# Instance normalisation over rows of 4096: an unrolled, tile-scheduled program rewritten as loops of three tiles with hand-placed semaphores

## Chip, cores, metric

One core of a Trainium2 chip. The metric is the time of one execution on the device in microseconds. A run is one execution; a median is over several. Runs of one call share a chip.

## The reference

```python
x: (256, 256, 4096) float32, eps = 1e-5
mean = np.mean(x, axis=2, keepdims=True)
var  = np.var(x, axis=2, keepdims=True)
return (x - mean) / np.sqrt(var + eps)
```

There are 65,536 rows. 1073.74 MB are read and as many written.

## The kernel before

A tile is 512 rows, four per partition, 64 KB in each of 128 partitions (8.39 MB). Three tiles are held at a time. Tile t is loaded, VectorE sums its rows, ScalarE squares the deviations and takes roots, both scale the tile in place, and it is stored. The last tile is cut in two. SyncE issues all transfers on one queue.

```python
K = 4; BUFS = 3
io = ctx.enter_context(tc.tile_pool(name="io", bufs=BUFS))
...
def load(i):
    x_tile = io.tile([P, K, d], fp32)
    keep(nc.sync.dma_start(out=x_tile[:, : spans[i][1], :], in_=rows(x_flat, spans[i])))
...
def mean(r):
    keep(nc.vector.tensor_reduce(out=part[:, r, :], in_=row, axis=AX.X, op=ALU.add))
    ...
# the order of issue
for i in range(BUFS):
    load(i)
for i in range(last + 1):
    compute(i)
    if i == last - 2:
        load(last)
    store(i)
    if 1 <= i < last - 2:
        load(i + 2)
```

The program is written out in full: 128 tiles, 2436 VectorE instructions.

## Time and profile before

| | before |
|---|---|
| median of the first three runs | 5013.53 us (5005.49 to 5014.84) |
| profiled run | 4995.86 us |
| VectorE, ScalarE busy | 68%, 50% |
| moved | 2147.5 MB, mean 430 GB/s |
| instruction fetch (queue 14) | 38 transfers, 0.31 MB |

The **busy share** is the time that transfers took over the time there was. The **rate** counts bytes. This is the line of rates in 40 slices of the page of before:

```profile
GB/s 426 430 433 431 434 434 432 435 435 433 433 436 434 433 434 433 434 432 432 429 428 433 431 429 433 429 430 429 434 425 427 428 429 429 427 428 428 428 433 391
```

### The profile page before, as it was taken

How to read it: one execution, taken by the hardware profiler on the slowest of the kernel's cores; microseconds unless marked ns; L12 is line 12 of the kernel's file. 1: busy time of each engine (PE TensorE's matmuls, PEld its weight loads, DVE VectorE, ACT ScalarE, POOL GpSimd, SP SyncE). 2: the span in 40 equal slices, each digit the busy share in tenths (PEclk: the TensorE clock that was granted, in tenths of full speed). 3: DMA queues.
4: the chain of work that ended last, by engine and by line, in shares of the span. 5: the costliest groups of instructions: out<-in, count | busy, mean ns of one | idle time of the engine just before them, and what ended most of it. 6: DMA issues, size and time to landing. Idle time of an engine off the chain costs nothing.

```text
span 4994.1 us, 4917 instructions
## 1 busy us (share of the span) xinstructions
DVE 3392.6 (68%) x2436; ACT 2501.4 (50%) x1413; POOL 0.2 (0%) x4
## 2 busy tenths in 40 slices
DVE  6666667766776667666667666766666666666666
ACT  4555445554455445554455544555445554455545
POOL 0000000000000000000000000000000000000000
DMA  9999999999999999999999999999999999999999
GB/s 426 430 433 431 434 434 432 435 435 433 433 436 434 433 434 433 434 432 432 429 428 433 431 429 433 429 430 429 434 425 427 428 429 429 427 428 428 428 433 391
DMA packets 37190, 2147.81 MB, mean 430 GB/s; under 512 B 4128, under 2 KB 4128, under 8 KB 4128
## 3 DMA queue, kind: packets, MB, share of 16 engines
q1 hardware_dynamic: 37152, 2147.50, 99.9%
q14 instruction: 38, 0.31, 0.0%
HBM read 1073.74 MB, written 1073.74 MB: 430 GB/s over the span
## 4 chain that ended last, share of the span: by engine, by line
DVE 53%; DMA 23%; another core or an unknown queue 20%; ACT 3%; issue 1%; SPq 0%; ACTq 0%
DVE part L74 37%; DMA x_tile<-in_x_dram 22%; DVE x_tile L95 12%; DVE nsum L75 2%; ACT junk L81 2%; ACT x_tile L103 2%; DVE nmean L76 1%; DMA out_dram<-x_tile 1%; DVE nbias L89 1%; DVE rstd L88 0%; SPq L118 0%; ACTq L159 0%; ACT L87 0%; ACT std L87 0%
## 5 line engine op out<-in xcount | busy, mean ns | idle before, releaser
L74 DVE TENSOR_REDUCE part<-x_tile 128x64 f32<-128x4096 f32 x512 | 2258.8, 4412 | 1520.3 <-DMA x_tile<-in_x_dram 1520.3
L81 ACT ACTIVATE junk<-x_tile,nmean 128x4096 f32<-128x4096 f32 x512 | 1883.0, 3678 | 2445.2 <-DVE nmean L76 2445.2
L95 DVE TENSOR_SCALAR x_tile<-x_tile,rstd,nbias 128x4096 f32<-128x4096 f32 x383 | 912.6, 2411 | 10.4 <-DVE nbias L89 1.1
L103 ACT ACTIVATE x_tile<-x_tile,nbias,rstd 128x4096 f32<-128x4096 f32 x129 | 488.5, 3787 | 0.1
L75 DVE TENSOR_REDUCE nsum<-part 128x1 f32<-128x64 f32 x512 | 112.7, 220 | 17.7
L81 ACT ACTIVATION_READ_ACCUMULATOR junk<-x_tile,nmean 128x1 f32 x512 | 95.5, 187 | 0.0
L76 DVE TENSOR_SCALAR nmean<-nsum 128x1 f32<-128x1 f32 x512 | 78.7, 154 | 17.5
L87 ACT ACTIVATE std<-ss,eps_tile 128x3 f32<-128x3 f32 (+1 forms) x258 | 76.2, 295 | 8.3
L88 DVE RECIPROCAL rstd<-std 128x3 f32<-128x3 f32 (+1 forms) x258 | 41.6, 161 | 8.6 <-ACT std L87 8.6
L89 DVE TENSOR_TENSOR nbias<-nmean,rstd 128x3 f32<-128x3 f32 (+1 forms) x258 | 41.5, 161 | 8.9
L81 ACT ACT_TABLE_LOAD x1 | 1.3, 1283 | 22.7 <-DMA x_tile<-in_x_dram 22.7
L87 ACT ACT_TABLE_LOAD x1 | 1.3, 1283 | 0.0
L49 DVE MEMSET eps_tile<- 128x1 f32 x1 | 0.1, 59 | 0.8 <-PEq L145 0.8
L145 POOL MEMSET const-bfloat16-1.0<- 128x1 bf16 x1 | 0.1, 102 | 0.0
L145 POOL MEMSET const-uint8-127<- 128x1 uint8 x1 | 0.1, 102 | 0.0
L145 POOL MEMSET const-float32-0.0<- 128x1 f32 x1 | 0.1, 99 | 0.2 <-issue 0.2
L145 POOL MEMSET const-float32-1.0<- 128x1 f32 x1 | 0.1, 99 | 0.0
## 6 DMA issues: line engine op xcount, KB each, us to landing
x_tile<-in_x_dram SPq DMA_DIRECT2D x2, 4096.0 KB, 30.7
out_dram<-x_tile SPq DMA_DIRECT2D x2, 4096.0 KB, 18.9
x_tile<-in_x_dram SPq DMA_DIRECT2D x127, 50.4
out_dram<-x_tile SPq DMA_DIRECT2D x127, 31.1
```

Source lines behind the costliest of these rows:

```text
L49: nc.vector.memset(eps_tile, eps)
L74: keep(nc.vector.tensor_reduce(out=part[:, r, :], in_=row, axis=AX.X, op=ALU.add))
L75: keep(nc.vector.tensor_reduce(out=nsum[:, c], in_=part[:, r, :], axis=AX.X, op=ALU.add, negate=True))
L76: keep(nc.vector.tensor_scalar_mul(out=nmean[:, c], in0=nsum[:, c], scalar1=1.0 / d))
L81: nc.scalar.activation(out=junk, in_=x_tile[:, r, :], func=AF.Square, bias=nmean[:, c], scale=1.0, accum_out=ss[:, c])
L87: keep(nc.scalar.activation(out=std[:, c], in_=ss[:, c], func=AF.Sqrt, bias=eps_tile, scale=1.0 / d))
L88: keep(nc.vector.reciprocal(out=rstd[:, c], in_=std[:, c]))
L89: keep(nc.vector.tensor_mul(out=nbias[:, c], in0=nmean[:, c], in1=rstd[:, c]))
L95: nc.vector.tensor_scalar(out=row, in0=row, scalar1=rstd[:, c], scalar2=nbias[:, c], op0=ALU.mult, op1=ALU.add)
L103: keep(nc.scalar.activation(out=row, in_=row, func=AF.Identity, bias=nbias[:, c], scale=rstd[:, c]))
L145: nc = _bacc.Bacc("TRN2", target_bir_lowering=False, num_devices=1)
```

## The change

The intent is a short program: each engine runs a loop over three tiles, waits on semaphores placed by hand, and the waiter resets each one, so that rounds need no barrier. Computation and its order stay. The core of the diff, cut:

```diff
-    io = ctx.enter_context(tc.tile_pool(name="io", bufs=BUFS))
+    X = [pool.tile([P, K, d], fp32, name=f"x{s}") for s in range(BUFS)]
+    loaded = [nc.alloc_semaphore(f"loaded{s}") for s in range(BUFS)]
...
+    def take(engine, sem, count):
+        engine.wait_ge(sem, count)
+        engine.sem_clear(sem)
...
+    def store(s, k, dst):
+        take(S, done[s], k)
+        S.dma_start(out=dst, in_=X[s][:, :k, :]).then_inc(stored[s], 16)
+    def load(s, k, src):
+        take(S, stored[s], 16)
+        S.dma_start(out=X[s][:, :k, :], in_=src).then_inc(loaded[s], 16)
...
-    for i in range(BUFS):
-        load(i)
-    for i in range(last + 1):
-        compute(i)
-        ...
+                load(0, K, x_t[0])
+                load(1, K, x_t[1])
+                with S.Fori(0, rounds * BUFS, BUFS) as i:
+                    for s in range(BUFS):
+                        store(s, K, out_t[bass.ds(i + s, 1)]...)
+                        load((s + 2) % BUFS, K, x_t[bass.ds(i + s + 2, 1)]...)
...
+                with V.Fori(0, rounds) as i:
+                    for s in range(BUFS):
+                        vector_tile(s, K)
...
+                with A.Fori(0, rounds) as i:
+                    for s in range(BUFS):
+                        scalar_tile(s, K)
```

Besides what it intends, the change loads two tiles at the start instead of three, and puts the tiles at byte 16544 of a partition instead of 16512.

More of the change, by code (lines that the diff above doesn't have):

```diff
@@ L18 @@
     nc = tc.nc
-    keep = tc.keep_in_program_order
     fp32 = mybir.dt.float32
@@ L32 @@
     assert n % (P * K) == 0 and d % C == 0
-    spans = [(t * P * K, K) for t in range(n // (P * K) - 1)]
-    spans += [(n - P * K, K // 2), (n - P * K // 2, K // 2)]
-    last = len(spans) - 1
-    def rows(flat, span):
-        r0, k = span
-        return flat[r0 : r0 + P * k, :].rearrange("(p k) d -> p k d", k=k)
-    io = ctx.enter_context(tc.tile_pool(name="io", bufs=BUFS))
-    small = ctx.enter_context(tc.tile_pool(name="small", bufs=4))
-    singles = ctx.enter_context(tc.tile_pool(name="singles", bufs=1))
+    ntiles = n // (P * K)
@@ L46 @@
+    x_t = x_flat.rearrange("(t p k) d -> t p k d", p=P, k=K)
+    out_t = out_flat.rearrange("(t p k) d -> t p k d", p=P, k=K)
+    half = K // 2
+    h0 = n - P * K
+    x_h = x_flat[h0:n, :].rearrange("(h p k) d -> h p k d", p=P, k=half)
+    out_h = out_flat[h0:n, :].rearrange("(h p k) d -> h p k d", p=P, k=half)
+    pool = ctx.enter_context(tc.tile_pool(name="pool", bufs=1))
     psum = ctx.enter_context(tc.tile_pool(name="psum", bufs=1, space=bass.MemoryType.PSUM))
-    eps_tile = singles.tile([P, 1], fp32)
@@ L49 @@
-    nc.vector.memset(eps_tile, eps)
+    eps_tile = pool.tile([P, 1], fp32)
     junk = psum.tile([P, d], fp32)
-    tiles = {}
-    def load(i):
-        x_tile = io.tile([P, K, d], fp32)
-        keep(nc.sync.dma_start(out=x_tile[:, : spans[i][1], :], in_=rows(x_flat, spans[i])))
-        tiles[i] = x_tile
-    def compute(i):
-        x_tile = tiles[i]
-        k = spans[i][1]
-        part = small.tile([P, K, C], fp32)
-        nsum = small.tile([P, K], fp32)
-        nmean = small.tile([P, K], fp32)
-        ss = small.tile([P, K], fp32)
-        std = small.tile([P, K], fp32)
-        rstd = small.tile([P, K], fp32)
-        nbias = small.tile([P, K], fp32)
-        def mean(r):
-            c = slice(r, r + 1)
-            row = x_tile[:, r, :].rearrange("p (c f) -> p c f", c=C)
-            keep(nc.vector.tensor_reduce(out=part[:, r, :], in_=row, axis=AX.X, op=ALU.add))
-            keep(nc.vector.tensor_reduce(out=nsum[:, c], in_=part[:, r, :], axis=AX.X, op=ALU.add, negate=True))
-            keep(nc.vector.tensor_scalar_mul(out=nmean[:, c], in0=nsum[:, c], scalar1=1.0 / d))
-        def square(r):
-            c = slice(r, r + 1)
-            keep(
-                nc.scalar.activation(
-                    out=junk, in_=x_tile[:, r, :], func=AF.Square, bias=nmean[:, c], scale=1.0, accum_out=ss[:, c]
-                )
-            )
-        def scales(c):
-            keep(nc.scalar.activation(out=std[:, c], in_=ss[:, c], func=AF.Sqrt, bias=eps_tile, scale=1.0 / d))
-            keep(nc.vector.reciprocal(out=rstd[:, c], in_=std[:, c]))
-            keep(nc.vector.tensor_mul(out=nbias[:, c], in0=nmean[:, c], in1=rstd[:, c]))
-        def apply_dve(r):
-            c = slice(r, r + 1)
-            row = x_tile[:, r, :]
-            keep(
-                nc.vector.tensor_scalar(
-                    out=row, in0=row, scalar1=rstd[:, c], scalar2=nbias[:, c], op0=ALU.mult, op1=ALU.add
-                )
-            )
-        def apply_act(r):
-            c = slice(r, r + 1)
-            row = x_tile[:, r, :]
-            keep(nc.scalar.activation(out=row, in_=row, func=AF.Identity, bias=nbias[:, c], scale=rstd[:, c]))
-        for r in range(k - 1):
-            mean(r)
-            square(r)
-        mean(k - 1)
-        scales(slice(0, k - 1))
-        square(k - 1)
-        for r in range(k - 2):
-            apply_dve(r)
-        scales(slice(k - 1, k))
-        apply_dve(k - 1)
-        apply_act(k - 2)
@@ L117, in store @@
-    def store(i):
-        keep(nc.sync.dma_start(out=rows(out_flat, spans[i]), in_=tiles.pop(i)[:, : spans[i][1], :]))
-    for i in range(BUFS):
-        load(i)
-    for i in range(last + 1):
-        compute(i)
-        if i == last - 2:
-            load(last)
-        store(i)
-        if 1 <= i < last - 2:
-            load(i + 2)
+    X = [pool.tile([P, K, d], fp32, name=f"x{s}") for s in range(BUFS)]
+    part = [pool.tile([P, K, C], fp32, name=f"part{s}") for s in range(BUFS)]
+    nsum, nmean, ss, std, rstd, nbias = (
+        [pool.tile([P, K], fp32, name=f"{name}{s}") for s in range(BUFS)]
+        for name in ("nsum", "nmean", "ss", "std", "rstd", "nbias")
+    )
@@ new lines @@
+    loaded = [nc.alloc_semaphore(f"loaded{s}") for s in range(BUFS)]
+    stored = [nc.alloc_semaphore(f"stored{s}") for s in range(BUFS)]
+    own_v = nc.alloc_semaphore("own_v")
+    own_a = nc.alloc_semaphore("own_a")
+    means = nc.alloc_semaphore("means")
+    stds = nc.alloc_semaphore("stds")
+    scaled = nc.alloc_semaphore("scaled")
+    done = [nc.alloc_semaphore(f"done{s}") for s in range(BUFS)]
+    ready = nc.alloc_semaphore("ready")
+    def take(engine, sem, count):
+        engine.wait_ge(sem, count)
+        engine.sem_clear(sem)
@@ new lines, with vector_tile, mine @@
+    V, A, S = nc.vector, nc.scalar, nc.sync
+    def vector_tile(s, k):
+        x = X[s]
+        own = 0
+        def mine(instruction):
+            nonlocal own
+            own += 1
+            return instruction.then_inc(own_v, 1)
+        take(V, loaded[s], 16)
+        for r in range(k):
+            c = slice(r, r + 1)
+            row = x[:, r, :].rearrange("p (c f) -> p c f", c=C)
+            mine(V.tensor_reduce(out=part[s][:, r, :], in_=row, axis=AX.X, op=ALU.add))
+            V.wait_ge(own_v, own)
+            mine(V.tensor_reduce(out=nsum[s][:, c], in_=part[s][:, r, :], axis=AX.X, op=ALU.add, negate=True))
+            V.wait_ge(own_v, own)
+            V.tensor_scalar_mul(out=nmean[s][:, c], in0=nsum[s][:, c], scalar1=1.0 / d).then_inc(means, 1)
+        for i, c in enumerate((slice(0, k - 1), slice(k - 1, k))):
+            if i == 0:
+                V.wait_ge(stds, 1)
+            else:
+                take(V, stds, 2)
+            mine(V.reciprocal(out=rstd[s][:, c], in_=std[s][:, c]))
+            V.wait_ge(own_v, own)
+            mine(V.tensor_mul(out=nbias[s][:, c], in0=nmean[s][:, c], in1=rstd[s][:, c]))
+            if i == 0:
+                V.wait_ge(own_v, own)
+                V.sem_inc(scaled, 1)
+            else:
+                take(V, own_v, own)
+            for r in range(0, k - 2) if i == 0 else (k - 1,):
+                c = slice(r, r + 1)
+                V.tensor_scalar(
+                    out=x[:, r, :], in0=x[:, r, :], scalar1=rstd[s][:, c], scalar2=nbias[s][:, c],
+                    op0=ALU.mult, op1=ALU.add,
+                ).then_inc(done[s], 1)
@@ new lines, in scalar_tile @@
+    def scalar_tile(s, k):
+        x = X[s]
+        for r in range(k):
+            c = slice(r, r + 1)
+            if r == k - 1:
+                A.wait_ge(own_a, k - 1)
+                A.activation(
+                    out=std[s][:, : k - 1], in_=ss[s][:, : k - 1], func=AF.Sqrt, bias=eps_tile, scale=1.0 / d
+                ).then_inc(stds, 1)
+                take(A, means, k)
+            else:
+                if r:
+                    A.wait_ge(own_a, r)
+                A.wait_ge(means, r + 1)
+            A.activation(
+                out=junk, in_=x[:, r, :], func=AF.Square, bias=nmean[s][:, c], scale=1.0, accum_out=ss[s][:, c]
+            ).then_inc(own_a, 1)
+        take(A, own_a, k)
+        c = slice(k - 1, k)
+        A.activation(out=std[s][:, c], in_=ss[s][:, c], func=AF.Sqrt, bias=eps_tile, scale=1.0 / d).then_inc(stds, 1)
+        c = slice(k - 2, k - 1)
+        take(A, scaled, 1)
+        A.activation(
+            out=x[:, k - 2, :], in_=x[:, k - 2, :], func=AF.Identity, bias=nbias[s][:, c], scale=rstd[s][:, c]
+        ).then_inc(done[s], 1)
@@ new lines, in store, with _ @@
+    def store(s, k, dst):
[4 more added lines that the diff above has]
+        S.dma_start(out=X[s][:, :k, :], in_=src).then_inc(loaded[s], 16)
+    rounds = (ntiles - 4) // BUFS
+    tail = [(t % BUFS, K, x_t[t], out_t[t]) for t in range(rounds * BUFS, ntiles - 1)]
+    tail += [((ntiles - 1 + h) % BUFS, half, x_h[h], out_h[h]) for h in range(2)]
+    with tc.tile_critical():
+        with nc.Block() as block:
+            @block.sync
+            def _(sync):
+                for s in range(BUFS):
+                    S.sem_inc(stored[s], 16)
+                load(0, K, x_t[0])
+                load(1, K, x_t[1])
+                with S.Fori(0, rounds * BUFS, BUFS) as i:
+                    for s in range(BUFS):
+                        store(s, K, out_t[bass.ds(i + s, 1)].rearrange("o p k d -> p (o k) d"))
+                        load((s + 2) % BUFS, K, x_t[bass.ds(i + s + 2, 1)].rearrange("o p k d -> p (o k) d"))
+                todo = tail[2:]
+                for t, (s, k, _, dst) in enumerate(tail):
+                    if t == len(tail) - 3:
+                        load(*todo.pop(0)[:3])
+                    store(s, k, dst)
+                    if todo:
+                        load(*todo.pop(0)[:3])
+                for s in range(BUFS):
+                    take(S, stored[s], 16)
+            @block.vector
+            def _(vector):
+                V.memset(eps_tile, eps).then_inc(ready, 1)
+                with V.Fori(0, rounds) as i:
+                    for s in range(BUFS):
+                        vector_tile(s, K)
+                for s, k, _, _ in tail:
+                    vector_tile(s, k)
+            @block.scalar
+            def _(scalar):
+                take(A, ready, 1)
+                with A.Fori(0, rounds) as i:
+                    for s in range(BUFS):
+                        scalar_tile(s, K)
+                for s, k, _, _ in tail:
+                    scalar_tile(s, k)
```

## The prediction

> **What bounds the kernel now.** I read the page from the top: busy shares, slices, queues, chain, groups; then the chain in order of time for the middle of the run, the timeline of the SP queue there, and the timeline of the first 120 us.
>
> The head of the page, its slices and its queues:
>
> ```profile
> span 4994.1 us, 4917 instructions
> DVE 3392.6 (68%) x2436; ACT 2501.4 (50%) x1413; POOL 0.2 (0%) x4
> DMA  9999999999999999999999999999999999999999
> DMA packets 37190, 2147.81 MB, mean 430 GB/s; under 512 B 4128, under 2 KB 4128, under 8 KB 4128
> q1 hardware_dynamic: 37152, 2147.50, 99.9%
> q14 instruction: 38, 0.31, 0.0%
> ```
>
> No engine is near full: VectorE stands at 68%, ScalarE at 50%. The row of nines and the 99.9% say that the 16 DMA engines have work throughout; 1073.74 MB in and the same out cannot be made smaller by this change. The kernel is a copy of 2147.5 MB at 430 GB/s with the arithmetic beside it. The chain of waits gives VectorE 53%, but it follows what released what and does not see a FIFO behind a busy wire; the group table shows what VectorE does between tiles:
>
> ```profile
> L74 DVE TENSOR_REDUCE part<-x_tile 128x64 f32<-128x4096 f32 x512 | 2258.8, 4412 | 1520.3 <-DMA x_tile<-in_x_dram 1520.3
> L95 DVE TENSOR_SCALAR x_tile<-x_tile,rstd,nbias 128x4096 f32<-128x4096 f32 x383 | 912.6, 2411 | 10.4 <-DVE nbias L89 1.1
> ```
>
> VectorE waits 1520.3 us for loads, over 126 waits 12.1 us a tile. The timeline in the middle of the run shows where that wait sits:
>
> ```profile
> 2518.42 0.33 SPq L118 DMA_DIRECT2D out_dram<-x_tile  x1
> 2518.80 0.43 SPq L57 DMA_DIRECT2D x_tile<-in_x_dram  x1
> 2530.01 4.42 DVE L74 TENSOR_REDUCE part<-x_tile 128x64 f32<-128x4096 f32 x1 [11.71 <-DMA x_tile<-in_x_dram]
> ...
> 2557.06 0.33 SPq L118 DMA_DIRECT2D out_dram<-x_tile  x1
> 2557.44 0.43 SPq L57 DMA_DIRECT2D x_tile<-in_x_dram  x1
> 2568.96 4.42 DVE L74 TENSOR_REDUCE part<-x_tile 128x64 f32<-128x4096 f32 x1 [12.01 <-DMA x_tile<-in_x_dram]
> ```
>
> One tile takes 38.95 us (2530.01 to 2568.96). A tile is 128 x 16384 x 4 = 8.39 MB each way, which is 19.5 us a transfer and 39.0 us a tile at 430 GB/s: the period is the traffic. From a tile's landing to its store's issue are 27.05 us (2530.01 to 2557.06). When a store is issued, the next load still needs 11.5 to 11.9 us to land. So the queue never runs dry, and **each tile has about 11.5 us of slack**: whatever the change adds between landing and store is hidden up to that.
>
> [...] a load's median time to landing is 50.4 us, which is the remaining 11.5 plus store 19.5 plus itself 19.5. [...] The listing of the built program has loop bodies of 71 instructions on VectorE, 40 on ScalarE and 20 on SyncE[...]. [...]
>
> **The change part by part.**
>
> 1. Unrolled program becomes loops. The instruction queue moved 0.31 MB; at 430 GB/s that is 0.7 us of wire. Removing most of it: -0.7 us. [...]
>
> 2. Semaphores. Per tile VectorE gets three wait-and-clear instructions and one separate increment; ScalarE three wait-and-clears and two split waits; SyncE two wait-and-clears and two fused address calculations. None was in the trace; my estimate is at most 0.2 us each (the shortest recorded operation, the mean's scaling at 154 ns, is the scale). Even were all 13 in series: 2.6 us, inside 11.5: 0. The waits on the engine's own work were there before, in the same places.
>
> 3. Activation tables. The built listing has two table loads inside ScalarE's loop body, before the first square and before the first root, where the unrolled program has two in all. At 1.28 us (the page's row) that is 82 x 1.28 = 105 us more ScalarE busy time, about 2606 us. The first of each round falls while ScalarE waits for VectorE's first mean (it sat idle 17 us there). The second lies between third square and root: it may delay every third tile by up to 1.3 us. With part 2 that is 3.9 us at worst, inside 11.5: 0.
>
> 4. **Start.** This isn't in the words of the change. Before issues three loads at once, then store 0. The changed program issues loads 0 and 1, then waits for tile 0, stores it, and only then issues load 2. The beginning of the trace of before:
>
> ```profile
> 0.73 1.34 SPq L57 DMA_DIRECT2D x_tile<-in_x_dram  x3
> 22.62 4.42 DVE L74 TENSOR_REDUCE part<-x_tile 128x64 f32<-128x4096 f32 x1 [21.77 <-DMA x_tile<-in_x_dram]
> 50.50 27.22 SPq L118 DMA_DIRECT2D out_dram<-x_tile  x2
> ```
>
> Load 0 needs 21.8 us on an empty queue (0.73 to 22.57), 2.3 more than its 19.5 of wire: start-up and completion. Load 1 lands at 22.6 + 19.5 = 42.1. In before load 2 then fills the wire to 61.6, past the store issued at 50.50. In the changed kernel nothing follows load 1; the store on an empty queue lands at 50.5 + 21.8 = 72.3 instead of 42.1 + 19.5 = 61.6. **The wire stands idle for 10.7 us.** From there the order is the same (store 0, load 2, store 1, load 3, ...), the slack of every tile is again 39.0 - 28 = 11, and nothing makes the gap up: the wire is the bound, and time lost on it is lost. +10.7 us. [...]
>
> 5. End. The last loads and stores have constant addresses and the order of before; at 4977.7, when the last store is issued, the wire still had about 5 us of the store ahead to do (the last store landed 15.5 us later for 9.8 us of wire). The extra semaphore work is hidden there. [...]
>
> Sum: -0.7 + 10.7 + 0.8 + 1.2 = +12.0 us. 5013.53 + 12.0 = 5025.5, taken as 5025.
>
> **The rivals.**
> - The compute chain becomes the bound. For: a store's address now comes from registers, waits are separate instructions, tables reload. Against: 11.5 us of slack, against 3.9 at worst. A loss of 2% is 100 us over 128 tiles, 0.8 us a tile beyond the slack, so 12.3 us of additions. Time then: over 5115. Chance 2%.
> - The transfer itself gets slower. The build puts the tiles at byte 16544 of a partition instead of 16512, so at a multiple of 32 rather than of 128, and a register address might give other descriptors. Against: the listing has the same shape, 128 rows of 64 KB, on the same queue[...]. A loss of 2% would show as 421 GB/s in all slices. Time then 5115. Chance 2 to 3%.
> - The start costs nothing, because the missing load is made up later. For: the queue holds 11 us of work in reserve. Against: reserve only prevents idling; it does not move bytes sooner. Time then 5014.
> - Removing the long program helps: [...] a tile lands only with its slowest engine. 0.31 MB on one engine of 27 GB/s would be 11.5 us, which could cancel the start. Against: 99.9% busy on all sixteen shows no engine waiting for a slow one. Time then 5014 as well. These two I give 20% together; they make the low side of the range.
>
> **Range and chances.** The three runs before lie from 5005 to 5015 and the profiled one took 4995.86, so a run moves by some 10 us either way. Centre 5025; low 5008 (rival three or four and a good run), high 5045 (the gap doubled by a slow entry or longer first tile, and a poor run). Two per cent is 100 us either way: faster is all but ruled out[...]; slower needs the first or second rival.
>
> **What would show it.** In the profile of the changed kernel: GB/s near 430 in all slices but the first; the first slice a tenth lower (10.7 of its 125 us); the first store issued at about 51 us and load 2 right behind it rather than at the start; VectorE's first wait for tile 2 long, until about 92 us; later waits for loads 9 to 12 us a tile (a wait near zero would show the compute chain as the bound, and be my error); table loads x82 or slightly more; instruction-queue bytes far below 0.31 MB. The prediction is wrong if the middle period is not 38.9 us, or if the start gap is there while the end does not move.

Three terms lose their lines: the branches (0), entering the block (+0.8) and leaving it (+1.2); the last two were the author's estimates, not worked out from a trace. The sum came to -0.7 + 10.7 + 0.8 + 1.2 = +12.0 us, so 5025; without the two it would be +10.0, so 5023.5. The 27 GB/s of one engine in the last rival is the page's 430 over 16 engines. Of the 2.3 us that load 0 takes over its wire time, 1.0 pass before its first piece starts, and 0.3 from the end of its last piece to VectorE's start.

## The result, and the profile after

| | before | after |
|---|---|---|
| runs of the first comparison | 5013.53, 5005.49, 5014.84, 5005.27 | 4975.0, 4975.37, 4974.48, 4977.38 |
| median | 5009.51 us | 4975.18 us |
| span of the profiled run | 4994.1 us | 4973.1 us |

The ratio is 0.9932 (95% interval 0.9914 to 0.9949): 0.7% faster. Ratios here are the mean time of one kernel's fast runs over that of the other's of the same rounds, so not quite the ratio of the medians. The changed kernel repeats within 3 us, while before moves by 10. The forecast was 5025, 5008 to 5045.

The head of the page of the changed kernel, its slices, queues and table loads:

```profile
span 4973.1 us, 6421 instructions
DVE 3396.3 (68%) x2436; ACT 2599.6 (52%) x1493; POOL 0.2 (0%) x4
GB/s 380 434 432 432 434 431 434 433 434 434 435 434 434 433 435 434 434 434 433 435 431 438 431 436 433 434 434 433 435 432 436 432 436 431 433 435 432 434 434 411
q1 hardware_dynamic: 37152, 2147.50, 99.8%
q14 instruction: 3, 0.02, 0.0%
L127 ACT ACT_TABLE_LOAD x41 | 52.6, 1283 | 2.0 <-DVE eps_tile L177 1.2
L119 ACT ACT_TABLE_LOAD x41 | 52.6, 1283 | 0.7
```

The first slice is lower than in before (380 against 426), as forecast; the later ones, but for the last, stay at 431 to 438, 434 on average, where before falls. The busy share is the same, 99.8% against 99.9%.

The start, from the timeline of the changed kernel, and then the wire in three stretches there (columns: stretch; length and VectorE busy with count; ScalarE; GpSimd; clock; DMA share; GB/s). A transfer counts in the stretch where it starts, so a share can exceed 1:

```profile
51.58 0.36 SPq L141 DMA_DIRECT2D out_dram<-x  x1
52.20 0.35 SPq L145 DMA_DIRECT2D x<-in_x_dram  x1
94.14 4.42 DVE L87 TENSOR_REDUCE part<-x 128x64 f32<-128x4096 f32 x1 [15.74 <-DMA x<-in_x_dram]
```

```profile
38.00:42.00 4.00, 4.00 (x1) 3.98 (x3) 0.00 (x0) 1.00 0.61 262
42.00:52.00 10.00, 8.80 (x11) 8.89 (x6) 0.00 (x0) 1.00 0.00 0
52.00:60.00 8.00, 7.93 (x4) 3.80 (x2) 0.00 (x0) 1.00 1.22 524
```

No transfer starts from 42 to 52 us: the forecast idle stretch is there. The rest of the run pays it back. The wire by stretches, first before, then after:

```profile
1200.00:2200.00 1000.00, 682.95 (x490) 500.05 (x283) 0.00 (x0) 1.00 1.00 434
2200.00:3200.00 1000.00, 676.73 (x484) 496.42 (x280) 0.00 (x0) 1.00 1.00 431
3200.00:4200.00 1000.00, 682.23 (x491) 504.29 (x286) 0.00 (x0) 1.00 1.00 429
4200.00:4800.00 600.00, 401.21 (x286) 292.34 (x165) 0.00 (x0) 1.00 1.00 428
```

```profile
1200.00:2200.00 1000.00, 685.75 (x492) 523.91 (x302) 0.00 (x0) 1.00 1.00 434
2200.00:3200.00 1000.00, 685.72 (x492) 525.21 (x303) 0.00 (x0) 1.00 1.00 434
3200.00:4200.00 1000.00, 684.94 (x492) 524.43 (x303) 0.00 (x0) 1.00 1.00 434
4200.00:4800.00 600.00, 416.97 (x301) 317.71 (x182) 0.00 (x0) 1.00 1.00 434
```

Until 2200 us the two are equal; from there before loses about 1%, with the DMA share at 1.00 in both. The middle of the changed kernel, to be set beside the prediction's lines of before:

```profile
2496.36 4.42 DVE L87 TENSOR_REDUCE part<-x 128x64 f32<-128x4096 f32 x1 [10.63 <-DMA x<-in_x_dram]
2523.79 0.35 SPq L141 DMA_DIRECT2D out_dram<-x  x1
2535.00 4.42 DVE L87 TENSOR_REDUCE part<-x 128x64 f32<-128x4096 f32 x1 [11.48 <-DMA x<-in_x_dram]
```

One tile takes 38.64 us there (2496.36 to 2535.00).

**Two readings from the records under the profile.** The trace has each transfer's duration and the 16 completion counts of each DMA, one per DMA engine. A piece of 64 KB, one partition of a tile, takes 2418 ns nearly always; sixteen engines at that pace make 16 x 65,536 B / 2.418 us = 434 GB/s. Some pieces take 2.6 to 3.6 us, a few up to 4.2; I call those over 2550 ns *stretched*. The time from the first to the last of the 16 completions of one DMA shows how far the fastest DMA engine is ahead of the slowest; I call it the *lead*. VectorE's first sum of a tile starts after the last of them, by 0.02 us in before and 0.13 in after (medians).

```
                 lead in us near (us)               stretched pieces of 32,512
              500  1000  2000  3000  4000     before 1000  1000-2000  after 2000
before        4.1   6.1   9.3   9.7  10.3         157         26         876
after         3.1   5.6   5.7   5.2   4.7         198          2          82
```

In both kernels the lead grows at first, while pieces are stretched. In after it stops at 5.7 us and hardly a piece is stretched for a thousand microseconds. In before it goes on to 10 us, and then stretched pieces become frequent and stay. The sums agree with the spans: an engine has 2064 pieces (the smaller ones of the last tile included) of mean 2416.8 ns in before, 4988 us of its 4994; in after they have mean 2403.6 ns, 4961 us of 4973. That is 27 us gained on the wire, less 6 of the larger remainder (the idle start, less what ends sooner), which is the 21 us between the spans.

So the question is why the 16 DMA engines of before drift to a lead of 10 us, and what of the change stops it. **Theory**, argued here and tested below: (a) the lead cannot exceed the slack, the time between the issue of a store and the landing of the next load, less some 1.3 us (in before 11.6 less a lead of 10.3), because a fast engine then has no work until the next issue; (b) in that capped condition pieces get stretched, and everything runs at the disturbed pace; (c) fetched instruction blocks push the engines towards it. In the trace of before a fetch of 8 KB takes 309 ns (median), and beside 35 of its 38 fetches a data piece under way is stretched by 0.1 to 0.65 us, which at moments chosen at random holds for 29%. **Rivals:** the semaphores and register addresses; SyncE's time between two issues; the new place of the tiles; the late third load.

### The profile page after: what moved, and what is told of

Its sections match the earlier page's. It is cut to its first block, busy times and chain, and to the rows that moved or that the text cites. A ratio compares the mean times of both kernels' runs of the same rounds, so it can differ in the third digit from the quotient of the medians.

```text
span 4973.1 us, 6421 instructions
## 1 busy us (share of the span) xinstructions
DVE 3396.3 (68%) x2436; ACT 2599.6 (52%) x1493; POOL 0.2 (0%) x4
## 3 DMA queue, kind: packets, MB, share of 16 engines
q1 hardware_dynamic: 37152, 2147.50, 99.8%
## 4 chain that ended last, share of the span: by engine, by line
DMA 74%; DVE 17%; ACT 7%; issue 1%; another core or an unknown queue 1%; SPq 0%; ACTq 0%; DVEq 0%
DMA x<-in_x_dram 42%; DMA out_dram<-x 32%; DVE part L87 16%; ACT junk L127 3%; ACT x L135 3%; DVE nsum L89 1%; DVE nmean L91 1%; DVE x L107 0%; ACTq L153 0%; SPq L141 0%; ACT std L132 0%; SPq L145 0%; ACTq L69 0%; ACT L119 0%
## 5 line engine op out<-in xcount | busy, mean ns | idle before, releaser
L87 DVE TENSOR_REDUCE part<-x 128x64 f32<-128x4096 f32 x512 | 2258.8, 4412 | 1438.2 <-DMA x<-in_x_dram 1438.2
L127 ACT ACTIVATE junk<-x,nmean 128x4096 f32<-128x4096 f32 x512 | 1882.2, 3676 | 2337.3 <-DVE nmean L91 2337.3
L107 DVE TENSOR_SCALAR x<-x,rstd,nbias 128x4096 f32<-128x4096 f32 x383 | 912.5, 2411 | 37.7 <-DVE nbias L99 16.0
L135 ACT ACTIVATE x<-x,nbias,rstd 128x4096 f32<-128x4096 f32 x129 | 488.5, 3787 | 0.0
L127 ACT ACTIVATION_READ_ACCUMULATOR junk<-x,nmean 128x1 f32 x512 | 95.5, 187 | 0.0
L132 ACT ACTIVATE std<-ss,eps_tile 128x1 f32<-128x1 f32 x129 | 38.0, 295 | 15.0
L119 ACT ACTIVATE std<-ss,eps_tile 128x3 f32<-128x3 f32 x129 | 38.2, 296 | 3.3
```

Source lines behind the costliest of these rows:

```text
L87: mine(V.tensor_reduce(out=part[s][:, r, :], in_=row, axis=AX.X, op=ALU.add))
L107: V.tensor_scalar(out=x[:, r, :], in0=x[:, r, :], scalar1=rstd[s][:, c], scalar2=nbias[s][:, c], op0=ALU.mult, op1=ALU.add,).then_inc(done ...
L119: A.activation(out=std[s][:, : k - 1], in_=ss[s][:, : k - 1], func=AF.Sqrt, bias=eps_tile, scale=1.0 / d).then_inc(stds, 1)
L127: A.activation(out=junk, in_=x[:, r, :], func=AF.Square, bias=nmean[s][:, c], scale=1.0, accum_out=ss[s][:, c]).then_inc(own_a, 1)
L132: A.activation(out=std[s][:, c], in_=ss[s][:, c], func=AF.Sqrt, bias=eps_tile, scale=1.0 / d).then_inc(stds, 1)
L135: A.activation(out=x[:, k - 2, :], in_=x[:, k - 2, :], func=AF.Identity, bias=nbias[s][:, c], scale=rstd[s][:, c]).then_inc(done[s], 1)
```

## The experiments

All kernels passed the comparison with the reference. Two are wrong in their arithmetic (they sum half a row) and pass the comparison all the same. The fetched blocks forecast for e4, e8 and e15 can be estimated from the page of before: 38 fetches for 4917 recorded instructions, 129 each, so 22 for 2900 and 4 for 500.

**1. The three loops written out** (e1_unrolled).

```diff
-                with V.Fori(0, rounds) as i:
-                    for s in range(BUFS):
-                        vector_tile(s, K)
+                for t in range(rounds * BUFS):
+                    vector_tile(t % BUFS, K)
   (the same on ScalarE and SyncE, with constant addresses)
```

> The changed kernel with its three loops written out: same hand-placed semaphores, same tile addresses, same late third load, but constant addresses and the whole program fetched. Theory 1 (instruction fetch: each fetched 8 KB block stretches a transfer on one DMA engine, and the engines drift apart until the fast ones run out of work): the fetch comes back, about 45 blocks, and the time goes to 5005 to 5022 us; the spread of the 16 landings of one transfer grows towards 10 us and the wire falls from 434 to about 430 GB/s after 2000 us. Theory 2 (semaphores or tile addresses made the gain): stays at 4975, within 5 us.

Measured 4999.88, 4999.99, 5005.08 and 5024.76 us, median 5002.54, beside before at 5006.22 (ratio 1.0014, 0.9982 to 1.0046): the gain is gone. 43 fetched blocks; the lead reaches 9.7 at 2000 us. The semaphores and the place of the tiles are as in the changed kernel, so they do not make the gain by themselves.

**2. The kernel before with the late third load** (e3_before_late_load).

```diff
-    for i in range(BUFS):
+    for i in range(BUFS - 1):
         load(i)
-        if 1 <= i < last - 2:
+        if 0 <= i < last - 2:
             load(i + 2)
```

> The kernel before with the third load issued after store 0, as the changed kernel does. Wire theory (time lost on the wire at the start is not made up): +8 to +12 us on before, 5017 to 5022. Rival (the order at the start is what kept the engines together in the changed kernel, so it makes the gain): 4975 to 4985. Rival (start is absorbed later): 5010.

Measured 4998.3 to 5021.28, median 5004.52, beside before at 5006.22; ratio 1.0009 (0.9979 to 1.004). My 8 to 12 us more are not shown, and the interval, 10 us down to 20 us up, is too wide to exclude them. What it does show is that the late load alone does not bring 4975: with the program written out as in before (38 fetches there), the lead still goes to 10.

**3. Fetch on an engine that is idle, and its control** (e4_sp_pad_unrolled, e5_sp_pad_loop).

```diff
   after each load on SyncE:
+                        for _ in range(20):
+                            S.sem_clear(spare)
   e4: SyncE written out; e5: the same inside its loop
```

> The changed kernel with loops on VectorE and ScalarE as they are, but SyncE written out, with 20 clears of an unused semaphore after each load: some 2900 instructions, about 22 fetched blocks of 8 KB, on an engine that is idle then. Theory 1: half the dose of before, so the gain shrinks: 4983 to 5000 us, landings spread to 7 to 10 us. Theory 2: 4975 within 3 us.

> Control of the former: the same 20 clears for each tile, but inside the loop, so that they run as often and are not fetched again. Every theory: 4975 within 3 us, and the spread of landings about 5.7 us as in the changed kernel. If it is as slow as the former, it is the clears themselves and not their fetch.

Written out: 5009.39 to 5018.37, median 5013.45, all four runs disturbed, with 26 fetched blocks. In the loop: 4978.03, 4982.07, 5012.56, 5017.58. The control missed its forecast: with the clears in the loop (the changed kernel, whose loop it is, has 3 fetches; those of e5 are not in the record), two of four runs were disturbed. So (c) has to be weakened: **there is a quiet condition and a disturbed one**; the second came in all four runs with fetch, but fetch need not be the only thing that can bring it (experiment 5 bears on this). Times between the two occur as well (before took 4985.7 to 5017.05 over all calls); a disturbance that sets in earlier or later would fit, but only one profile per kernel was kept, so this is not shown. Also the time does not follow the dose: 26 blocks cost no less than 38.

**4. The changed kernel again** (after_again, no edit).

> The changed kernel once more, because its padded control fell to 4978 to 5018 us without any fetch. If the changed kernel has one regime: all runs 4974 to 4978. If fetch is only one of several things that push the engines out of a quiet pattern (theory 1b), some runs lie at 5000 to 5018, clearly apart from the rest.

Six runs, 4974.95 to 4975.92, beside before at 5011.34 (ratio 0.9933, 0.9918 to 0.9949). With the first comparison, ten of ten runs are quiet. It isn't luck. In this run's trace the lead stands at 5.6 us until 3000 us and then rises to 8.0 at 4675, with 6 pieces stretched after 2000: the engines can drift in a quiet run too, without loss.

**5. Three loads at once in the looped kernel** (e2_three_loads).

```diff
-                load(0, K, x_t[0])
-                load(1, K, x_t[1])
+                for t in range(BUFS):
+                    load(t, K, x_t[t])
+                store(0, K, out_t[0])
   (the loop then stores tile i+s+1 and loads tile i+s+3)
```

> The changed kernel with the third load issued at once, as before does. Wire theory: 10.7 us less than the changed kernel in the same regime, 4964.5 in the quiet one, and about 5000 in a disturbed run. Rival (the late third load is what keeps the pattern quiet): 5000 to 5015 in most runs.

Five runs at 5004.34 to 5012.2 and one at 4963.94; median 5007.78, beside before at 5011.34. With the loops of the changed kernel (3 fetches there), but with all loads at once, it is mostly disturbed: the lead reaches 8.2 us near 1000 and stretched pieces become frequent from there:

```profile
200.00:1200.00 1000.00, 689.01 (x494) 527.86 (x304) 0.00 (x0) 1.00 1.00 433
1200.00:2200.00 1000.00, 676.43 (x483) 513.51 (x295) 0.00 (x0) 1.00 1.00 430
2200.00:3200.00 1000.00, 678.80 (x488) 523.12 (x302) 0.00 (x0) 1.00 1.00 428
```

The one quiet run is 11.1 us under the changed kernel of the same call (4975.05), which is the predicted cost of the late load, seen in the quiet condition on one run. So loops and late load are **both** needed, as long as the slack stays at 11 us and nothing else is changed (experiments 7 to 9 find other ways):

| | fetch (written out) | loops |
|---|---|---|
| three loads at once | before, 5006.22 | e2, 5007.78 (1 of 6 runs quiet) |
| third load late | e3, 5004.52; e1, 5002.54 | changed kernel, 4975.05 |

(The loops column is from the second call, where before had 5011.34; the other from the first.)

**6. Less slack and more slack** (e9_after_less_slack, e7_before_more_slack). These test (a) and (b); the transfers stay, and so do the fetches: 3 in e9 as in the changed kernel, 38 in e7 as in before.

```diff
   e9, changed kernel, VectorE:
+            if r == 0:
+                mine(V.tensor_reduce(out=part[s][:, r, :], in_=row, axis=AX.X, op=ALU.add))
+                V.wait_ge(own_v, own)
   e7, kernel before (wrong on purpose):
-            row = x_tile[:, r, :].rearrange("p (c f) -> p c f", c=C)
+            row = x_tile[:, r, : d // 2].rearrange("p (c f) -> p c f", c=C)
```

> The changed kernel with one row sum done twice in each tile: 4.4 us more between landing and store, slack 7 us, same result. Theory with a cap: the lead is capped at about 5.7 us, which the quiet pattern just needs, so long transfers appear through the whole run and the time goes to 4995 to 5020. Queue view: hidden, 4975 to 4980.

> Wrong result on purpose: the kernel before, but VectorE sums half of each row only, 4 x 2.2 = 8.8 us less per tile between landing and store, so that the slack grows from 11.5 to about 20 us. Fetch and all transfers as before. Theory 1 with a cap (an engine's lead over the slowest cannot exceed the slack less about 1.3 us; before reaches that cap of 10 us after 1700 us, and only then transfers lengthen): the lead is free to grow beyond 10 us, long transfers become rare, and the time falls to 4960 to 4975. Queue view of my prediction (slack only has to be above zero): no effect, 5005 to 5012.

With less slack: 5042.62 to 5045.55, **69 us slower than the changed kernel**, though VectorE stays idle before each tile. The timeline of e9 in the middle shows the slack from the store's issue, 2518.03 to 2525.40, which is 7.4 us, and 6.9 at the next tile (2557.28 to 2564.17); the median, to the landing itself, is 6.8:

```profile
2518.03 0.35 SPq L144 DMA_DIRECT2D out_dram<-x  x1
2518.64 0.34 SPq L148 DMA_DIRECT2D x<-in_x_dram  x1
2525.40 4.42 DVE L88 TENSOR_REDUCE part<-x 128x64 f32<-128x4096 f32 x1 [7.60 <-DMA x<-in_x_dram]
...
2557.28 0.35 SPq L144 DMA_DIRECT2D out_dram<-x  x1
2557.88 0.34 SPq L148 DMA_DIRECT2D x<-in_x_dram  x1
2564.17 4.42 DVE L88 TENSOR_REDUCE part<-x 128x64 f32<-128x4096 f32 x1 [7.16 <-DMA x<-in_x_dram]
```

Not all of the 69 us is the theory's. By the records, stretched pieces account for 46 us a DMA engine between the two profiled runs, and idle time between 200 and 4850 us for 9. The other 13 lie before 200 and after 4850 us, where the extra row sum is exposed because the queue is empty. The rate falls early; the wire of e9, then of e7, by stretches:

```profile
200.00:1200.00 1000.00, 789.41 (x508) 516.05 (x296) 0.00 (x0) 1.00 1.00 431
1200.00:2200.00 1000.00, 794.12 (x516) 524.12 (x303) 0.00 (x0) 1.00 1.00 428
```

```profile
1200.00:2200.00 1000.00, 465.83 (x491) 499.96 (x284) 0.00 (x0) 1.00 1.00 434
2200.00:3200.00 1000.00, 461.41 (x486) 491.44 (x279) 0.00 (x0) 1.00 1.00 431
```

With more slack: 4981.29 to 4993.02, median 4985.72, beside before at 5011.34 (ratio 0.9952, 0.993 to 0.9973). It is faster, but not to my 4960 to 4975 (the profiled run, 4993.02, is its slowest), and my estimate of the slack was off: it grew to 16.4 us, not 20; ScalarE's work was left as it was. The lead shows why the gain is partial:

```
                       slack   lead near 500  1000  2000  3000  4000   stretched pieces set in
e9 after, less slack    6.8             3.0   5.3   5.1   5.0   4.6    near 750
before                 11.6             4.1   6.1   9.3   9.7  10.3    near 2000
e7 before, more slack  16.4             6.1   9.1  12.8  14.5  14.6    near 2000 to 2500
```

In all three the lead grows and stops some 1.3 to 1.8 us under the slack, and the stretched pieces become frequent as it comes near. That is what (a) and (b) say. There is no one lead at which stretching starts: 9 us is harmless in e7 and cannot occur in e9. My forecast that the lead would settle by itself in e7 was wrong: with the fetch it did not settle.

A rival to slack was not run alone: e7, e9 and e10 also change how much VectorE reads of the tiles, and that could stretch the pieces. The traces speak against it. After 2000 us VectorE is busy during 57% of the time of stretched pieces in before and 59% in e9, less than during all pieces (69% and 81%); in e7 it is 54% against 48%. Experiment 9 has more slack with the arithmetic unchanged, and is quiet.

**7. More slack in the looped kernel** (e10_three_loads_more_slack: experiment 5 with the half sums, wrong).

> Wrong result on purpose: three loads at once, loops, and half of each row summed, so that the slack is about 16.4 us and the lead of an engine may grow to 14.7 instead of 10. Cap theory: without fetch the lead stops growing once no two engines disturb each other, if there is room for it: all or nearly all runs 4962 to 4967, landings spread constant below 14. Rival (with all three loads at once it never settles, only the late load settles it): 4980 to 5010 as with the fetch.

4969.83 to 4973.33, median 4970.09, ratio 0.9946 (0.9932 to 0.9959) to before at 4999.44. Five of five runs lie far below the median of 5007.78 of experiment 5 (another call). It lies 3 us over my range, since the lead crept up after 2500 us (12.8 at 4675) and 90 pieces were stretched after 2000. So the three loads at once do not forbid the quiet condition when there is room for the lead.

**8. The engines lined up once** (e13_three_loads_drain: experiment 5 with one wait).

```diff
                 store(0, K, out_t[0])
+                S.wait_ge(stored[0], 16)
```

> Three loads at once, loops, and SyncE waits once, for store 0 to land, before it issues store 1: the wire runs empty once for about 3 us[...]. If lining up at the start is what the late load contributes: 4966 to 4970 in most runs. If not: 5004 to 5012 as with three loads alone.

4967.33 to 4970.99 in five runs and 4976.85 in one; median 4969.21, ratio 0.9946 (0.9933 to 0.9958). With one wait added all six runs lie far below the five disturbed ones of experiment 5 (another call and chip; experiment 5 was not run again beside it), and the lead near 1000 us is 4.0 instead of 8.2. So running the wire empty once can take the place of the late load. That it does so by lining the engines up is argued, not shown: when the wire empties, the lead is only about 1 us, in experiment 5 as here (1.3 and 1.0 us at 83 us); what differs is that it then grows more slowly. This is the fastest correct kernel here; it beats before by 0.54% in this call, and experiment 10, the changed kernel but for its addresses, by 6.8 us in the same call.

**9. Loads in halves** (e11_half_loads), an attempt at a correct kernel with more slack.

```diff
-        S.dma_start(out=X[s][:, :k, :], in_=src).then_inc(loaded[s], 16)
+        S.dma_start(out=X[s][:, :half, :], in_=src[:, :half, :]).then_inc(loaded[s], 16)
+        if k > half:
+            S.dma_start(out=X[s][:, half:, :], in_=src[:, half:, :]).then_inc(loaded_b[s], 16)
```

> Correct result: three loads at once, loops, each load issued as two halves of two rows so that VectorE starts on the first half while the second lands; the time from the last landing to the store shrinks by some 9 us and the slack grows to about 20. Cost on the wire: 8 more transfers of 32 KB per engine and tile at 1213 ns against half of 2418, 64 ns a tile, 8 us in all. Cap theory: quiet in nearly all runs, 4970 to 4976. Rival (never settles with three loads): 4990 to 5015.

4982.43 to 4983.74: steady and quiet (15 stretched pieces after 2000 us), but 7 us over my range. The lead grows in an even line from 4.4 at 1000 to 15.8 at 4000 with hardly a stretched piece, so one engine is a little slower at this pattern: of the 16 completions near 4000 us, fifteen come within 4.1 us, and the last 11.5 us after them. The records also tell where the time went: the profiled run is 14.5 us over that of e13, 8.2 of it longer transfer time, as estimated (a piece of 32 KB takes 1213 ns in before and after, so two take 8 ns more than one of 64 KB), and 6.3 more idle time of the DMA engines. After 4850 us they are idle 17 us on average, against 6 in e13: at the end the fast engines have nothing left while the slowest finishes, so a lead that costs nothing on the way is paid there.

**10. The place of the tiles** (e6_aligned: the tiles allocated first, at byte 16512).

> The changed kernel with its three tiles allocated first, so at byte 16512 of a partition as in before, not 16544. Address rival (the new place of the tiles is needed for the quiet pattern): 5000 or more. Every other theory: 4975 within 3 us.

4975.53 to 4976.56, median 4975.99: as the changed kernel. The address rival falls.

**11. Fetch or SyncE's timing** (e8_dve_unrolled: VectorE's loop alone written out; e15_sp_unrolled: SyncE's alone, nothing added).

> The changed kernel with VectorE's loop alone written out: SyncE keeps its loop, its register addresses and the time between its two issues. About 2900 VectorE instructions, some 22 fetched blocks of 8 KB. Fetch theory: disturbed in most runs, 4990 to 5020. Rival (the register-addressed issues and their spacing on SyncE make the quiet pattern, and writing out SyncE is what lost it in the other two): 4975 within 3 us.

> The changed kernel with SyncE's loop alone written out, nothing added: constant addresses and the shorter spacing of store and load issue (0.45 us instead of 0.61), but only about 500 SyncE instructions, 4 fetched blocks. Fetch theory: mostly quiet, 4974 to 4980, perhaps one run disturbed. Rival (issue spacing): 5000 to 5020 in all runs.

In this call before lies at 4993.16, and the changed kernel was not run. VectorE written out: 4996.3 to 5006.23, median 5005.02, ratio 1.0012 (0.9986 to 1.0038): disturbed in all four, with SyncE as it was. SyncE written out: 4979.15 to 4981.27, median 4980.12, ratio 0.9968 (0.9943 to 0.9993): quiet in all four, 4 to 6 us over what the changed kernel took. Its issues are 0.45 us apart instead of 0.61 and its addresses constant, so these do not bring the disturbed condition. Queue 14 of the two:

```profile
q14 instruction: 24, 0.20, 0.0%
```

```profile
q14 instruction: 7, 0.06, 0.0%
```

VectorE's rates fall where those of before do:

```profile
1200.00:2200.00 1000.00, 681.09 (x489) 520.35 (x300) 0.00 (x0) 1.00 1.00 434
2200.00:3200.00 1000.00, 681.98 (x491) 525.45 (x304) 0.00 (x0) 1.00 1.00 430
```

The same arithmetic, the same semaphores and the same slack (11.1 us in both), with the fetch added (24 against 3): this is the cleanest run for (c). VectorE's loop branches went at the same time, and that was not tested by itself.

## Why the prediction was wrong

- *The wire is the bound*: right. *The kernel is a copy at 430 GB/s*: **wrong, and this is the step that failed.** I took the mean of before for the wire's own rate. The wire's rate with no stretched piece is 434; the mean of 430 is about 433 in the first half and 429 after. The period of 38.95 us that I measured at 2530 us was already a disturbed one; the changed kernel has 38.64 there (2496.36 to 2535.00), which is the sign of being wrong that I had named. Over the some 72 tiles that before had left after 2200 us, 0.31 us is 22 us. The best slices of that page, 434 to 436, lie 1% over the mean, which is some 50 us, and I counted none of it.
- *Removing the long program helps*: I listed this rival, gave it and another 20% together, and sized it as at most 11.5 us, the time of the fetched bytes on one engine. The direct time is indeed small (38 x 0.31 us, 35 of them with a stretched piece beside them), and with loop bodies of 71, 40 and 20 instructions there were 3 fetches in the whole run. What costs is that with the fetch the lead does not settle, and then pieces are stretched: 27 us a DMA engine, on average, between the two profiled runs. I argued against it with *99.9% busy shows no engine waiting*. That is the wrong view: a stretched piece is busy. The rates on the same page showed it.
- *Slack of 11.5 us hides what is added*: the changed kernel needs 27.4 us from landing to store (2496.36 to 2523.79) instead of 27.05, and that did no harm. But the rule is wrong in general: e9 added 4.4 us, still inside the slack, and lost 69 us, 55 of them in stretched pieces and idle time in the middle. Slack is also the room that the engines have to drift in.
- *Start, +10.7 us*: right in size. The idle stretch is there from 42 to 52 us, the first load is issued at 1.27 us instead of 0.73 and store 0 at 51.58 instead of 50.50, the DMA engines are idle 11.3 us more than in before in the first 200 us, and the quiet run of e2 is 11.1 us faster. I said that nothing makes the gap up. Without it the loops are mostly disturbed (e2, 5007.78), and e13 shows that a shorter empty moment is enough, so the gap brought in more than it cost. By what means is not shown.
- *Tables and semaphores: 0*: right. 82 table loads, ScalarE 2599.6 us against 2606 forecast. The *+1.2* for the end, an estimate of mine without a measured basis, did not come: after 4850 us the DMA engines are idle 5 us, against 8 in before. Two readings were off, without consequence: the shortest recorded operation is a memset of 59 ns, not 154, and the wait from the store's issue to the load's landing is 11.6 us in the lines shown, not 11.5.
- *Faster by 2% is all but ruled out, slower needs a rival*: within 2% is what came. The range, 5008 to 5045, failed because it was built around the spread of before, without asking why before spread by 10 us at all. The changed kernel, whose wire is steady, repeats within 1 us (after_again).

**What stays open.** Why a piece is stretched is not shown. Of those of before after 2000 us, 382 of 876 end 20 to 22 us after the issue of a store. Engines in step that disturb each other would fit, but no run measured it alone. Nor is it shown why, at a slack of 11 us, three loads at once settle only after a drain, or why the twenty clears of e5 disturbed two runs of four.

## What to carry to other kernels

When a kernel is bound by its transfers, read GB/s in stretches, not the busy share, and ask for the rate of the best stretch before taking the mean as the limit; here a fall over the run, and a time that varied from run to run, were the signs that there was something to gain. The sixteen engines that share each transfer drifted apart here, by 5 to 16 us. Three things went with quiet or quieter runs: more slack, which gives the lead room; one moment with an empty queue at the start; and loops, which take away most of the instruction fetch (38 to 3 transfers). Test such a condition with many runs: the same kernel can fall either way (e2: 4963.94 and 5012.2).
